# Second matrix of the three MLPs by block products of seven, first matrix's low parts by accumulating DMAs

## The chip, the cores and the metric

One core of one Trainium2 chip runs the kernel. The metric is the device time of one execution in microseconds; a kernel's time is the median of several runs. One execution was also recorded by the hardware profiler.

## What is computed

256 tokens of width 1024 pass through one block of a first kind and two of a second kind. Each block ends with an MLP of width 4096, and only these three MLPs change here:

```python
x = x + jnp.square(jax.nn.relu(h2 @ w_up[l])) @ w_down[l]              # first block
hid = jnp.square(jax.nn.relu(jnp.einsum('bsd,df->bsf', x, w_ff1)))     # each of the two others
ff = jnp.einsum('bsf,fd->bsd', hid, w_ff2)
return layernorm(DEEPNORM_ALPHA * x + ff, ln2_g, ln2_b)
```

All arrays are fp32. The first matrix is 1024x4096, the second 4096x1024.

## The kernel before

**Products in three parts.** Every fp32 operand is split into a high part, rounded to the engine's fp32r, and a low part, the rest. `mm3` (L319) then issues high x high, high x low and low x high: three matmuls (L320 to L322) for each block of 128 contracted rows.

**The weight stream.** All weights come from one packed array in the order of a plan (`build_plan`). A chunk is 128 x 2048 numbers and comes in two halves of 128x1024, 512 KB each. `Stream.load` has SP issue the loads into a ring of `RB` = 5 raw buffers. `Stream.piece` (L205) splits one half: ACT casts the raw half to the high part (`whi`, L213), then DVE subtracts it from the raw half to give the low part (`wlo`, L214). The split parts go to `NB` = 5 chunk buffers, and in an MLP `W.lend` adds a sixth. A chunk's buffer is free when PE has ended its last product with it (`W.free`).

**What sets the order.** The engines' queues are written in program order, with no scheduler. Between products the code calls `tick`, which advances the "sides" (generators with transposes and splits of other data) and pumps one or two pieces, if a buffer is free in program order. Each engine works its queue strictly in turn, so an instruction that waits holds all that stands behind it.

**An MLP.** Four chunks of the first matrix make hidden columns 0 to 1023 with the tokens on the partitions (these hidden columns are transposed by PE afterwards). The other twelve, here called up4 to up15, make 256 hidden columns each with the hidden columns on the partitions (`stream_a`): 48 matmuls of 128x256. ACT then applies relu and square (L800, L801), and the hidden block is split into high (ACT, L312) and low (DVE, L306). The second matrix is used in groups g of 512 hidden columns: `down(g, n, t, w)` multiplies the hidden block of token half t with the chunk of columns half n, 12 matmuls of 128x512. Each chunk serves both token halves, so 24 matmuls. The sums of all eight groups stay in four PSUM banks until the end, when `half` adds them to the residual in `xtok` and, in the second kind of block, makes the layer norm (`ln_half`, L912). Groups 0 to 5 run two groups behind up4 to up15, and groups 6 and 7 form a last round of four chunks, which are all held while each token half passes.

Of the kernel before, what the change touches and what calls it, by code (L numbers as in the profile page):

```python
# [9 lines left out]
F32 = mybir.dt.float32  # L10
# [6 lines left out]
D = 1024  # L17
S = 256
DFF = 4096
NB = 5  # L20
RB = 5
# [47 lines left out]

C2 = {}  # L70
# [7 lines left out]
def build_plan():  # L78

    plan = []  # L80
# [6 lines left out]

    def mlp(tag, wu, wd, l):
        for n in range(2):
            for j in range(2):  # L90
                wb((tag, "up", n, j), wu, l, 512 * n, 4 * j)
        for g in range(2, 8):
            for c in (2 * g, 2 * g + 1):
                wa((tag, "up", c), wu, l, 256 * c)
            for n in range(2):
                wb((tag, "dn", g - 2, n), wd, l, 512 * n, 4 * (g - 2))
        for n in range(2):
            for g in (6, 7):
                wb((tag, "dn", g, n), wd, l, 512 * n, 4 * g)
# [50 lines left out]

def pack_weights(inputs):

    plan = build_plan()
    flat = np.empty(sum(128 * k * n for _, _, _, _, k, _, n in plan), np.float32)
    o = 0
    for _, w, l, r0, k, c0, n in plan:
# [9 lines left out]
class Stream:  # L166
    def __init__(self, nc, raw_pool, w_pool, flat):
        self.nc, self.raw_pool, self.w_pool, self.flat = nc, raw_pool, w_pool, flat
        self.plan = [(p[0], p[4], p[6]) for p in build_plan()]
        self.dma_i = self.split_i = self.used = self.freed = self.off = 0  # L170
        self.raws, self.tiles = {}, {}
        self.main = []
        self.extra = None
        self.extra_used = -1

    def lend(self, pool, last):

# [1087 lines left out]
```

## Time and profile before

| | |
|---|---|
| Median of 3 runs | 1223.91 us (1223.78 to 1224.0) |
| The profiled execution's own time | 1223.95 us |
| Its span, first to last instruction | 1222.1 us |
| PE busy | 1208.5 us, 99% |
| DVE busy | 734.8 us, 60% |
| ACT busy | 631.6 us, 52% |
| DMA queue of SP (the weights) | 211.12 MB, 51.6% of 16 engines' span |
| Granted TensorE clock | 0.997 of 2.4 GHz |

A page of the profile gives the busy time of each engine and the chain of work that ended last, followed back from the last instruction. Groups of instructions have a line, an engine, an operation, output and input by name, their count, the busy sum, the mean of one, and the idle time before them with its releaser. The timeline has the start of each instruction or run of equal ones and how long it took. Matmuls overlap in the records, so their pace is read from start to start.

### The profile page before, as it was taken

Reading aid. Unit: us, or ns where it says so; the run is one execution under the profiler, and the core shown is the slowest. Engines: PE = TensorE matmul, PEld = TensorE weight load, DVE = VectorE, ACT = ScalarE, POOL = GpSimd, SP = SyncE. Lnnn points to the kernel's source line nnn. Section 1 sums busy time; section 2 is a strip of 40 time slices with the busy share of each in tenths; the row PEclk is TensorE's granted clock in tenths of the full one; section 3 lists DMA queues with packets and bytes.
Section 4 is the critical chain, followed back from the end, with each engine's and each line's share of the span. In section 5 each row is a group of like instructions: output and inputs, shape, how many; then the busy total and the mean of one; then the engine's idle time right before and its main releaser. Section 6 shows DMA issues by size and latency. Waiting matters only on the chain.

```text
span 1222.1 us, 18186 instructions
## 1 busy us (share of the span) xinstructions
PE 1208.5 (99%) x7365; PEld 1059.1 (87%) x7365; DVE 734.8 (60%) x941; ACT 631.6 (52%) x887; POOL 26.2 (2%) x45
## 2 busy tenths in 40 slices
PE   8999999999999999999999999999999999999997
PEld 5999987887888888998898889899889888989985
DVE  6488775656666655355476685535567668553452
ACT  6556555545454565455255556545535555653540
POOL 1000000000000000000000100000000010000000
PEclk9999999999999999999999999999999999999999
DMA  8644446665455565556444366555545436655530
GB/s 327 224 148 144 140 156 211 233 195 162 138 172 189 184 243 208 172 172 214 156 166 139 124 214 226 197 188 173 207 130 187 146 118 216 225 193 203 167 126 35
DMA packets 60468, 218.99 MB, mean 179 GB/s; under 512 B 6848, under 2 KB 6992, under 8 KB 60384
## 3 DMA queue, kind: packets, MB, share of 16 engines
q1 hardware_dynamic: 58320, 211.12, 51.6%
q0 software_dynamic: 1776, 6.38, 1.8%
q8 instruction: 58, 0.95, 0.3%
q10 hardware_dynamic: 288, 0.33, 0.1%
q14 instruction: 26, 0.21, 0.0%
HBM read 216.75 MB, written 1.05 MB: 178 GB/s over the span
## 4 chain that ended last, share of the span: by engine, by line
PE 95%; DVE 1%; ACT 1%; DMA 1%; issue 0%; DVEq 0%; POOLq 0%; SPq 0%; ACTq 0%
PE acc L320 17%; PE acc L322 17%; PE acc L321 17%; PE bank L320 13%; PE bank L322 13%; PE bank L321 13%; PE acc L402 2%; PE acc L333 2%; PE aux L329 1%; DMA raw<-in_wpack_dram 1%; PE aux L1082 0%; DMA gmix<-in_g_mix_dram 0%; DVE wlo L214 0%; PE aux L515 0%; PE aux L322 0%
## 5 line engine op out<-in xcount | busy, mean ns | idle before, releaser
L214 DVE TENSOR_TENSOR wlo<-raw,whi 128x1024 fp32r<-128x1024 f32 x392 | 465.0, 1221 | 116.6 <-ACT whi L213 114.5
L213 ACT CAST whi<-raw 128x1024 fp32r<-128x1024 f32 x392 | 394.6, 1048 | 108.7 <-PE bank L322 58.0
L320 PE MATMUL acc<-xTh,whi 128*128 128x256 f32 x1088 | 310.6, 285 | 0.0
L321 PE MATMUL acc<-xTl,whi 128*128 128x256 f32 x1088 | 307.7, 283 | 0.0
L322 PE MATMUL acc<-xTh,wlo 128*128 128x256 f32 x1088 | 307.5, 283 | 0.0
L320 PEld LDWEIGHTS acc<-xTh,whi 128*128 128x128 f32 x1088 | 207.9, 191 | 2.7 <-issue 1.0
L321 PEld LDWEIGHTS acc<-xTl,whi 128*128 128x128 f32 x1088 | 207.9, 191 | 1.0
L322 PEld LDWEIGHTS acc<-xTh,wlo 128*128 128x128 f32 x1088 | 208.0, 191 | 0.0
L320 PE MATMUL bank<-whi,hid 128*128 128x512 f32 x384 | 151.4, 394 | 0.0
L322 PE MATMUL bank<-whi,hid 128*128 128x512 f32 x384 | 151.3, 394 | 0.0
L321 PE MATMUL bank<-wlo,hid 128*128 128x512 f32 x384 | 151.2, 394 | 0.0
L306 DVE TENSOR_TENSOR hid<-r,hid 128x512 fp32r<-128x512 f32 x36 | 24.9, 692 | 166.2 <-ACT hid L312 166.2
L800 ACT ACTIVATE r<-acc 128x512 f32<-128x512 f32 x36 | 21.5, 598 | 147.1 <-PE acc L322 147.1
L320 PE MATMUL acc<-whi,xTh 128*128 128x512 f32 x224 | 90.6, 404 | 0.7 <-ACT xTh L312 0.7
L321 PE MATMUL acc<-wlo,xTh 128*128 128x512 f32 x224 | 88.2, 394 | 1.1 <-DVE wlo L214 1.1
L322 PE MATMUL acc<-whi,xTl 128*128 128x512 f32 x224 | 88.3, 394 | 0.0
L322 PEld LDWEIGHTS bank<-whi,hid 128*128 128x128 f32 x384 | 72.2, 188 | 16.9
L320 PEld LDWEIGHTS bank<-whi,hid 128*128 128x128 f32 x384 | 72.3, 188 | 15.9
L321 PEld LDWEIGHTS bank<-wlo,hid 128*128 128x128 f32 x384 | 72.2, 188 | 16.0
L320 PE MATMUL bank<-whi,xTh 128*128 128x512 f32 (+2 forms) x192 | 68.7, 358 | 0.0
L321 PE MATMUL bank<-wlo,xTh 128*128 128x512 f32 (+2 forms) x192 | 68.1, 354 | 0.0
L322 PE MATMUL bank<-whi,xTl 128*128 128x512 f32 (+2 forms) x192 | 68.0, 354 | 0.0
(263 smaller groups left out, 1457.6 us busy)
## 6 DMA issues: line engine op xcount, KB each, us to landing
raw<-in_wpack_dram SPq DMA_DIRECT2D x388, 512.0 KB, 4.4
raw<-in_wpack_dram SPq DMA_DIRECT2D x4, 528.0 KB, 4.3
gb<-in_ln_g_dram POOLq DMA_DIRECT2D x4, 512.0 KB, 3.9
bb<-in_ln_b_dram POOLq DMA_DIRECT2D x4, 512.0 KB, 6.1
x<-in_x_dram SPq DMA_DIRECT2D x3, 512.0 KB, 7.0
mem<-in_mem_dram SPq DMA_DIRECT2D x2, 512.0 KB, 6.5
out_dram<-x SPq DMA_DIRECT2D x4, 256.0 KB, 2.2
cst<-in_c_dram POOLq DMA_DIRECT2D x1, 898.0 KB, 7.0
```

Of the source, the lines that this page charges most:

```text
L213: nc.scalar.copy(hi, raw)
L214: nc.vector.tensor_tensor(lo, raw, hi.bitcast(F32), op=ALU.subtract)
L306: nc.vector.tensor_tensor(o, x, y, op=op)
L320: nc.tensor.matmul(o, lhsT=lh, rhs=rh, start=first, stop=False, skip_group_check=True)
L321: nc.tensor.matmul(o, lhsT=lh, rhs=rl, start=False, stop=False, skip_group_check=True)
L322: nc.tensor.matmul(o, lhsT=ll, rhs=rh, start=False, stop=last, skip_group_check=True)
L329: nc.tensor.matmul(o[:, h, :], lhsT=q[a][hs[h]], rhs=k[b][hs[h]], start=i == 0, stop=i == 2, skip_group_check=True)
L333: nc.tensor.matmul(o, lhsT=l, rhs=r, start=first, stop=last, skip_group_check=True)
L402: nc.tensor.transpose(o[:, k * 128:(k + 1) * 128], src[:, k * 128:(k + 1) * 128], ident)
L800: nc.scalar.activation(dst, src, AF.Relu)
```

## The change

The second matrix is cut, for each pair of groups (1024 hidden columns, "pair" 0 to 3), into four quarters of 512x512: q0 and q1 of the first group (columns half 0, half 1), q3 and q2 of the second. In pairs 0 and 2 the four outputs (two token halves by two column halves) are made of seven block products instead of eight. `PRODUCTS` lists them in their order: 1, 5, 6, 3, 7, 2, 4, here P1, P5, P6, P3, P7, P2, P4. Each has a chunk of its own, made of the raw quarters: P1 is q0, P5 is q0 = q0 + q1, P6 is q0 = q0 + q2, P3 is q2, P7 is q1 = q1 + q2, P2 is q3, P4 is q3 = q3 + q0. The sums are made in place in the raw buffers by DVE (`Stream.add`, L234). Each product also has an operand of its own, made from the hidden quarters (`seven_side`: four differences on DVE, seven splits on ACT and DVE). A product is 12 matmuls of 128x512. P1, P6, P7 and P4 accumulate on one PSUM bank ("A"), P5 and P3 on a second ("C"), P2 has a third ("B"). After each product `gather` adds or subtracts the bank as it then stands to a block of `xtok` (a DVE instruction with `xtok` and the bank as inputs, L353), so the next product on that bank comes after the gather. Pairs 1 and 3 keep the eight products; pair 1 is gathered into `xtok` too, pair 3 ends in `half`.

The order of an MLP is now: four first chunks; up4 to up7; seven products of pair 0; up8 to up11; the four chunks of pair 1; up12 to up15; seven products of pair 2; the four chunks of pair 3.

For the halves of up4 to up15, DVE makes no low part any more. ACT writes the negated high part into `wlo` (L251), and GpSimd issues a DMA (L252) that reads the weights again from the packed array and adds them onto `wlo`. The raw half is then free after ACT's cast.

`NB` is 4 in place of 5, with no lent buffer, and `RB` is 8 in place of 5. The four quarters of a pair are eight raw halves and stay in the ring until their last use.

```diff
-NB = 5
-RB = 5
+NB = 4
+RB = 8
...
+PRODUCTS = ((1, 0, None), (5, 0, 1), (6, 0, 2), (3, 2, None), (7, 1, 2), (2, 3, None), (4, 3, 0))
...
+    def w7(key, w, l, k0, c0, c1):
+        quarters = [(w, l, 128 * (k0 + 4 * i), 4, (c0, c1)[j], 512) for i, j in ((0, 0), (0, 1), (1, 1), (1, 0))]
+        for name, q, s in PRODUCTS:
+            plan.append(((*key, name), quarters if q == 0 and s is None else None, q, s))
...
-        for g in range(2, 8):
-            for c in (2 * g, 2 * g + 1):
+        for pair in range(1, 4):
+            for c in range(4 * pair, 4 * pair + 4):
                 wa((tag, "up", c), wu, l, 256 * c)
+            if pair % 2:
+                w7((tag, "dn", pair - 1), wd, l, 8 * (pair - 1), 0, 512)
             for n in range(2):
-                wb((tag, "dn", g - 2, n), wd, l, 512 * n, 4 * (g - 2))
-        for n in range(2):
-            for g in (6, 7):
-                wb((tag, "dn", g, n), wd, l, 512 * n, 4 * g)
+                for g in (2, 3) if pair == 2 else (6, 7) if pair == 3 else ():
+                    wb((tag, "dn", g, n), wd, l, 512 * n, 4 * g)
...
-    def lend(self, pool, last):
-
-        self.extra = (pool, [p[0] for p in self.plan].index(last))
-        self.extra_used = -1
-
-    def slot(self, c):
-        if self.extra is not None and c <= self.extra[1] and self.extra_used < self.freed:
-            return 2
-        return 1 if len(self.main) < NB or self.main[-NB] < self.freed else 0
...
-        return c < len(self.plan) and (h == 1 or self.slot(c) > 0)
+        return c < len(self.plan) and (h == 1 or c < NB + self.freed)
...
+        while self.dma_i < 2 * len(self.loads):
+            i, h = divmod(self.dma_i, 2)
+            j, g = divmod(self.dma_i - upto, 2)
+            if j >= 0 and 2 * self.last[j] + g >= self.split_i:
+                return
...
+    def add(self):
+        if self.added == self.split_i and self.added < 2 * len(self.plan):
+            c, h = divmod(self.added, 2)
+            _, _, _, q, s = self.plan[c]
+            if s is not None:
+                a, b = self.raws[2 * q + h], self.raws[2 * s + h]
+                self.nc.vector.tensor_tensor(a, a, b, op=ALU.add)
+            self.added += 1
     def piece(self):
         nc = self.nc
         c, h = divmod(self.split_i, 2)
-        m = self.plan[c][1] * self.plan[c][2] // 2
+        _, k, n, q, _ = self.plan[c]
+        m = k * n // 2
         if h == 0:
-            p = self.w_pool
-            if self.slot(c) == 2:
-                p, self.extra_used = self.extra[0], c
-            else:
-                self.main.append(c)
-            self.tiles[c] = tuple(p.tile([128, WMAX], F32R, tag=t, name=t) for t in ("whi", "wlo"))
+            self.tiles[c] = tuple(self.w_pool.tile([128, WMAX], F32R, tag=t, name=t) for t in ("whi", "wlo"))
         hi, lo = (t[:, h * m:(h + 1) * m] for t in self.tiles[c])
-        raw = self.raws.pop(self.split_i)
+        self.add()
+        raw = self.raws[2 * q + h]
         nc.scalar.copy(hi, raw)
-        nc.vector.tensor_tensor(lo, raw, hi.bitcast(F32), op=ALU.subtract)
         self.split_i += 1
+        self.add()
+        if self.by_dma(self.plan[c][0]):
+            nc.scalar.mul(lo, hi.bitcast(F32), -1.0)
+            nc.gpsimd.dma_start(lo, self.srcs[2 * q + h], accum_op=ALU.add)
+        else:
+            nc.vector.tensor_tensor(lo, raw, hi.bitcast(F32), op=ALU.subtract)
         self.load()
+    @staticmethod
+    def by_dma(key):
+        return len(key) == 3 and key[1] == "up"
...
+        def seven_side(pair):
+            x = hf[pair]
+            q = {(i, j): x[:, 4 * j:4 * j + 4, 128 * i:128 * i + 128] for i in range(2) for j in range(2)}
+            r = hp.tile([128, D], F32, tag="r", name="r", bufs=2)
+            d, e = (r[:, 512 * i:512 * i + 512].rearrange("p (k t) -> p k t", k=4) for i in range(2))
+            def put(name, src):
+                o = new_op(7)
+                split(o[0], o[1], src)
+                ops[pair, name] = o
+            put(1, q[0, 0])
+            tt(d, q[1, 1], q[1, 0], ALU.subtract)
+            yield
+            put(5, d)
+            stt(e, d, -1.0, q[0, 0], ALU.mult, ALU.subtract)
+            yield
+            put(6, e)
+            stt(d, e, -1.0, q[0, 1], ALU.mult, ALU.subtract)
+            yield
+            put(3, d)
+            tt(e, q[0, 0], q[1, 0], ALU.subtract)
+            yield
+            put(7, e)
+            yield
+            put(2, q[0, 1])
+            yield
+            put(4, q[1, 1])
...
+        def gather(i, j, bank, op):
+            x = xtok[:, i, 512 * j:512 * j + 512]
+            stt(x, x, alpha if (i, j) not in first else 1.0, bank, ALU.mult, op)
+            first.add((i, j))
+        def seven(pair):
+            bk = {}
+            for name, _, _ in PRODUCTS:
+                while (pair, name) not in ops:
+                    tick(0)
+                x = ops[pair, name]
+                c = "A" if name in (1, 6, 7, 4) else "B" if name == 2 else "C"
+                fresh = c not in bk
+                if fresh:
+                    bk[c] = bank()
+                w = W.get((tag, "dn", pair, name))
+                for k in range(4):
+                    mm3(bk[c], x[0][:, k, :], x[1][:, k, :], w[0][:, k, :], w[1][:, k, :], fresh and k == 0, k == 3)
+                    if k == 1:
+                        tick()
+                W.free()
+                for i, j, op in {1: ((0, 0, ALU.add),), 5: ((1, 1, ALU.subtract),), 6: ((0, 1, ALU.subtract),),
+                                 3: ((0, 1, ALU.subtract),), 7: ((1, 1, ALU.subtract),), 2: ((0, 0, ALU.add),),
+                                 4: ((1, 0, ALU.add),)}[name]:
+                    gather(i, j, bk[c], op)
+                tick()
...
+        for pair in range(1, 4):
+            for c in range(4 * pair, 4 * pair + 4):
+                p = stream_a((tag, "up", c), xT)
...
+            if pair % 2:
+                seven(pair - 1)
+            if pair == 2:
+                for n in range(2):
+                    p = [bank(), bank()]
+                    for g in (2, 3):
+                        w = W.get((tag, "dn", g, n))
+                        for t in range(2):
+                            down(p[t], n, g, t, w)
+                            if t:
+                                W.free()
+                            if g == 3:
+                                gather(t, n, p[t], ALU.add)
+                            tick()
```

In the counts of the two programs, matmuls of 128x512 on `bank` go from 1920 to 1848. On DVE, low parts of weights (128x1024) go from 388 to 352, 48 sums of raw halves (128x1024) are new, instructions on `xtok` with a bank (128x512) go from 24 to 78, and in place of 48 low parts of hidden blocks (128x512) stand 42 of 128x512 and 48 of 128x256 with 24 differences (128x512). On ACT, casts of weights go from 388 to 424, and 72 negated copies (128x1024) are new. On GpSimd 72 DMAs are new. SP's loads stay 392.

DVE around the first products of the second matrix in the first MLP. Before, from the split of up5's hidden block to that of up6's:

```order
L306 TENSOR_TENSOR hid_4083<-r,hid_4082 128x512 [waits Activation_49]
L214 TENSOR_TENSOR wlo<-raw,whi 128x1024 [waits DMAHW7_49,Activation_49]
L214 TENSOR_TENSOR wlo<-raw,whi 128x1024 [waits DMAHW0_49,Activation_49]
L214 TENSOR_TENSOR wlo<-raw,whi 128x1024 [waits DVE_49,DMAHW1_49,PE_49,Activation_49]
L214 TENSOR_TENSOR wlo<-raw,whi 128x1024 [waits DMAHW2_49,Activation_49]
L214 TENSOR_TENSOR wlo<-raw,whi 128x1024 [waits DMAHW3_49,DVE_49,Activation_49]
L214 TENSOR_TENSOR wlo<-raw,whi 128x1024 [waits DMAHW4_49,Activation_49]
L306 TENSOR_TENSOR hid_4301<-r,hid_4300 128x512 [waits PE_49,Activation_49]
```

Now, from the sum of P7's first half to the third gather (`x_3502<-x_3502,bank` rows are gathers, `raw<-raw` rows are sums of raw halves, `op` rows are splits of operands):

```order
L234 TENSOR_TENSOR raw<-raw 128x1024
L254 TENSOR_TENSOR wlo<-raw,whi 128x1024 [waits Activation_49]
L353 SCALAR_TENSOR_TENSOR x_3502<-x_3502,bank 128x512 [waits PE_49]
L350 TENSOR_TENSOR op_4390<-hf,op_4390 128x512 [waits Activation_49]
L234 TENSOR_TENSOR raw<-raw 128x1024
L254 TENSOR_TENSOR wlo<-raw,whi 128x1024 [waits Activation_49] x2
L353 SCALAR_TENSOR_TENSOR x_3502<-x_3502,bank 128x512 [waits PE_49]
L254 TENSOR_TENSOR wlo<-raw,whi 128x1024 [waits DMAHW1_49,Activation_49]
L234 TENSOR_TENSOR raw<-raw 128x1024 [waits DVE_49]
L254 TENSOR_TENSOR wlo<-raw,whi 128x1024 [waits DMAHW2_49,Activation_49]
L353 SCALAR_TENSOR_TENSOR x_3502<-x_3502,bank 128x512 [waits PE_49]
```

Before, nothing on DVE read a PSUM bank among these products; now a gather that waits for PE stands between the splits and sums, behind those that the code pumped earlier.

DVE at the end of the first MLP's second set of seven. Before, from the split of up15's hidden block into the last round:

```order
L306 TENSOR_TENSOR hid_5093<-r,hid_5092 128x512 [waits Activation_49]
L214 TENSOR_TENSOR wlo<-raw,whi 128x1024 [waits DMAHW7_49,Activation_49]
L214 TENSOR_TENSOR wlo<-raw,whi 128x1024 [waits DMAHW0_49,Activation_49]
L214 TENSOR_TENSOR wlo<-raw,whi 128x1024 [waits DVE_49,DMAHW1_49,PE_49,Activation_49]
L214 TENSOR_TENSOR wlo<-raw,whi 128x1024 [waits DMAHW2_49,Activation_49]
```

Now, from the sum for P4's second half to the gather of P2 (the gathers here are those of P3, P7 and P2):

```order
L234 TENSOR_TENSOR raw<-raw 128x1024 [waits DVE_49]
L254 TENSOR_TENSOR wlo<-raw,whi 128x1024 [waits Activation_49] x2
L353 SCALAR_TENSOR_TENSOR x_3502<-x_3502,bank 128x512 [waits PE_49]
L254 TENSOR_TENSOR wlo<-raw,whi 128x1024 [waits DMAHW3_49,Activation_49]
L254 TENSOR_TENSOR wlo<-raw,whi 128x1024 [waits DMAHW4_49,Activation_49]
L353 SCALAR_TENSOR_TENSOR x_3502<-x_3502,bank 128x512 [waits PE_49]
L254 TENSOR_TENSOR wlo<-raw,whi 128x1024 [waits DMAHW5_49,Activation_49]
L254 TENSOR_TENSOR wlo<-raw,whi 128x1024 [waits DMAHW6_49,Activation_49]
L353 SCALAR_TENSOR_TENSOR x_3502<-x_3502,bank 128x512 [waits PE_49]
```

Two low parts for the first chunk of pair 3, with loads of their own to wait for, now stand between the gather of P3 and that of P7.

ACT at the splits of the chunks up8 and up9 in the first MLP. Before:

```order
L312 CAST hid_4498<-r 128x512 [waits Activation_49]
L213 CAST whi<-raw 128x1024 [waits DMAHW5_49]
L213 CAST whi<-raw 128x1024 [waits DMAHW6_49]
L800 ACTIVATE r<-acc 128x512 [waits DVE_49,PE_49]
L801 ACTIVATE r<-r 128x512 [waits Activation_49]
L312 CAST hid_4498<-r 128x512 [waits Activation_49]
```

Now, behind the casts of P4's halves:

```order
L247 CAST whi<-raw 128x1024 [waits DVE_49]
L247 CAST whi<-raw 128x1024 [waits DMAHW3_49,PE_49,Activation_49]
L251 ACTIVATE wlo<-whi 128x1024 [waits DMASW7_49,DMASW6_49,Activation_49]
L247 CAST whi<-raw 128x1024 [waits DMAHW4_49]
L251 ACTIVATE wlo<-whi 128x1024 [waits Activation_49]
L247 CAST whi<-raw 128x1024 [waits DMAHW5_49,PE_49]
L251 ACTIVATE wlo<-whi 128x1024 [waits DMASW1_49,DMASW0_49,Activation_49]
```

Each half of these chunks has a second ACT instruction, and GpSimd's queue has one DMA for each; here from up8's first half to up10's first half:

```order
L252 DMA wlo<-in_wpack_dram 128x1024 [waits DMASW0_49,DMASW6_49,DVE_49,DMASW7_49,PE_49,Activation_49]
L252 DMA wlo<-in_wpack_dram 128x1024 [waits DMASW1_49,Activation_49]
L252 DMA wlo<-in_wpack_dram 128x1024 [waits DVE_49,DMASW2_49,PE_49,Activation_49]
L252 DMA wlo<-in_wpack_dram 128x1024 [waits DMASW3_49,Activation_49]
L252 DMA wlo<-in_wpack_dram 128x1024 [waits DVE_49,DMASW4_49,PE_49,Activation_49]
```

A half of up8 is whole when this DMA has landed, where before it was whole after DVE's subtraction.

## Rows read from the trace of the kernel before

**Rows 1.** The page: busy us, share and instructions of each engine; PE clock by slice.

```profile
PE 1208.5 (99%) x7365; PEld 1059.1 (87%) x7365; DVE 734.8 (60%) x941; ACT 631.6 (52%) x887; POOL 26.2 (2%) x45
...
PEclk9999999999999999999999999999999999999999
```

**Rows 2.** The page: the chain that ended last, shares of the span by engine.

```profile
PE 95%; DVE 1%; ACT 1%; DMA 1%; issue 0%; DVEq 0%; POOLq 0%; SPq 0%; ACTq 0%
```

**Rows 3.** Waits of PE, longest in total first: us in total, times, longest us.

```profile
PE acc L402 <- DVE ht L309: 1.3, 1, 1.3
PE acc L321 <- DVE wlo L214: 1.1, 1, 1.1
```

**Rows 4.** Stretches in the first two MLPs: length, busy us (instructions) by engine, clock, DMA share, GB/s.

```profile
440.00:620.00 180.00, 180.00 (x1116) 161.68 (x1115) 92.18 (x99) 86.70 (x108) 0.54 (x1) 1.00 0.52 176
700.00:890.00 190.00, 190.00 (x1127) 168.19 (x1126) 106.72 (x115) 103.04 (x130) 2.19 (x4) 1.00 0.60 204
```

**Rows 5.** Timeline of PE in the first MLP: start us, us, what, count.

```profile
442.08 0.29 PE L320 MATMUL acc<-xTh,whi 128*128 128x256 f32 x1
...
447.85 0.28 PE L320 MATMUL acc<-xTh,whi 128*128 128x256 f32 x1
...
450.72 1.03 PE L402 MATMUL acc<-ident,r 128*128 128x128 f32 x8
451.51 0.36 PE L320 MATMUL acc<-xTh,whi 128*128 128x256 f32 x1
...
454.46 0.39 PE L320 MATMUL bank<-whi,hid 128*128 128x512 f32 x1
...
460.96 0.39 PE L321 MATMUL bank<-wlo,hid 128*128 128x512 f32 x1
```

**Rows 6.** Groups by line and shape: count, busy us, mean ns of one, idle before.

```profile
L214 DVE TENSOR_TENSOR wlo<-raw,whi 128x1024 fp32r<-128x1024 f32 x388 | 460.1, 1220 | 116.0 <-ACT whi L213 113.8
L213 ACT CAST whi<-raw 128x1024 fp32r<-128x1024 f32 x388 | 390.4, 1048 | 106.2 <-PE bank L322 58.0 <-issue 15.9 <-PE acc L322 15.9
L306 DVE TENSOR_TENSOR hid<-r,hid 128x512 fp32r<-128x512 f32 x36 | 24.9, 692 | 166.2 <-ACT hid L312 166.2
L916 DVE SCALAR_TENSOR_TENSOR x<-x,bank 128x512 f32<-128x512 f32 x16 | 11.0, 684 | 30.2 <-PE bank L322 30.2
L306 DVE TENSOR_TENSOR mixl<-acc,mixh 128x256 fp32r<-128x256 f32 x8 | 3.4, 422 | 5.0 <-ACT mixh L312 4.7
L801 ACT ACTIVATE r<-r 128x512 f32<-128x512 f32 x48 | 30.4, 633 | 1.5
L800 ACT ACTIVATE r<-acc 128x512 f32<-128x512 f32 x36 | 21.5, 598 | 147.1 <-PE acc L322 147.1
L312 ACT CAST mixh<-acc 128x256 fp32r<-128x256 f32 x8 | 3.0, 373 | 14.7 <-PE acc L333 14.7
```

**Rows 7.** Timeline of DVE in the first MLP.

```profile
452.38 1.29 DVE L306 TENSOR_TENSOR hid<-acc,hid 128x512 fp32r<-128x512 f32 x2 [0.20 <-ACT hid L312]
...
457.56 5.76 DVE L214 TENSOR_TENSOR wlo<-raw,whi 128x1024 fp32r<-128x1024 f32 x5 [0.26 <-ACT whi L213]
```

**Rows 8.** DMA issues: out<-in queue op xcount, KB each, median us to landing.

```profile
raw<-in_wpack_dram SPq DMA_DIRECT2D x388, 512.0 KB, 4.4
gb<-in_ln_g_dram POOLq DMA_DIRECT2D x4, 512.0 KB, 3.9
bb<-in_ln_b_dram POOLq DMA_DIRECT2D x4, 512.0 KB, 6.1
```

**Rows 9.** Stretches at the kernel's start: as rows 4.

```profile
6.00:10.00 4.00, 2.19 (x12) 0.95 (x10) 2.32 (x5) 1.84 (x5) 0.55 (x1) 0.99 1.02 408
10.00:20.00 10.00, 8.71 (x32) 6.12 (x32) 8.85 (x10) 6.97 (x10) 2.30 (x4) 0.83 1.00 386
```

**Rows 10.** Timeline of PE at the kernel's start.

```profile
12.30 0.63 PE L321 MATMUL acc<-wlo,xTh 128*128 128x512 f32 x1
12.73 0.63 PE L322 MATMUL acc<-whi,xTl 128*128 128x512 f32 x1
```

More of the change, by code (lines that the diff above doesn't have):

```diff
@@ L148, in build_plan, with build_loads @@
     return plan
+def build_loads():
+    loads, chunks = [], []
+    for p in build_plan():
+        if len(p) == 7:
+            chunks.append((p[0], p[4], p[6], len(loads), None))
+            loads.append(p[1:])
+            continue
+        key, quarters, q, s = p
+        if quarters is not None:
+            base = len(loads)
+            loads.extend(quarters)
+        chunks.append((key, 4, 512, base + q, None if s is None else base + s))
+    return loads, chunks
 def pack_weights(inputs):
-    plan = build_plan()
-    flat = np.empty(sum(128 * k * n for _, _, _, _, k, _, n in plan), np.float32)
+    loads = build_loads()[0]
+    flat = np.empty(sum(128 * k * n for _, _, _, k, _, n in loads), np.float32)
     o = 0
-    for _, w, l, r0, k, c0, n in plan:
+    for w, l, r0, k, c0, n in loads:
         for h in range(2):
@@ L186, in room @@
+        self.last = [0] * len(self.loads)
+        for c, (_, _, _, q, s) in enumerate(self.plan):
+            self.last[q] = c
+            if s is not None:
+                self.last[s] = c
+        self.dma_i = self.split_i = self.added = self.used = self.freed = self.off = 0
+        self.raws, self.srcs, self.tiles = {}, {}, {}
     def room(self):
         c, h = divmod(self.split_i, 2)
-        return c < len(self.plan) and (h == 1 or self.slot(c) > 0)
+        return c < len(self.plan) and (h == 1 or c < NB + self.freed)
@@ L786, in block_kernel, with mlp @@
     yst.close()
-    def mlp(tag, xT, half, on_start):
+    def mlp(tag, xT, half, on_start, xtok, alpha):
         st = ExitStack()
@@ new lines, in mlp @@
+        first = set()
+        def gather(i, j, bank, op):
[23 more added lines that the diff above has]
+                tick()
@@ L910, in cc_, with ln_half @@
         return c2s["cst"][:, C2[n][0]:C2[n][1]]
-    def ln_half(t, n, bank, xtok, gb, bb, xT, cell, tmp, fin=None):
+    def ln_half(t, n, bank, xtok, gb, bb, xT, cell, tmp, fin=None, alpha=ALPHA):
         ns = slice(512 * n, 512 * n + 512)
@@ L915, in ln_half @@
             cell[t] = sm.tile([128, 2], F32, tag="lsum", name="lsum")
-        nc.vector.scalar_tensor_tensor(out=xtok[:, t, ns], in0=xtok[:, t, ns], scalar=ALPHA, in1=bank, op0=ALU.mult,
+        nc.vector.scalar_tensor_tensor(out=xtok[:, t, ns], in0=xtok[:, t, ns], scalar=alpha, in1=bank, op0=ALU.mult,
                                        op1=ALU.add, accum_out=cell[t][:, n:n + 1])
@@ L1221, in mlp_half @@
                 ln_half(t, n, bank, xtok, gb2[0], gb2[1], None, cellf, tmp,
[L1222 removed]
+                        lambda t, hs: nc.sync.dma_start(out[0, t * 128:(t + 1) * 128, hs], xtok[:, t, hs]), 1.0)
                 return
```

88 lines of the change are left out of this document (44 added, 44 removed).

## The prediction, made before the changed kernel was run

> **What bounds the kernel now.** I read the page's busy shares first: PE works 1208.5 us of 1222.1, at the full clock in every slice [rows 1]. The chain that ended last is PE for 95% [rows 2], and PE's waits for other engines are single ones of 1.3 us and less [rows 3]. Then the stretches inside the MLPs: PE is busy 180.00 us of 180, while DVE has 92.18 and ACT 86.70 [rows 4]. So in an MLP the time is the number of matmuls times their pace. DVE and ACT have room on average; whether they have it at each place is another question, and the change puts their work in bursts.
>
> The pace comes from starts [rows 5]: 48 matmuls of 128x256 take 447.85 - 442.08 = 5.77 us, one chunk of up4 to up15. Of 128x512, 28 take 460.96 - 454.46 = 6.50 us, 0.232 each, so a product of 12 takes 2.79. Eight transposes take 0.79.
>
> **What is removed.** 1920 - 1848 = 72 matmuls of 128x512, all on the path: 72 x 0.232 = 16.7 us.
>
> **DVE's prices.** Alone: 1.220 us for a low part (128x1024), 0.692 for 128x512, 0.684 for the form of a gather, 0.422 for 128x256 [rows 6]. In a row they are closer: five low parts in 5.76 us are (5.76 - 1.22)/4 = 1.14 apart, two of 128x512 in 1.29 are 0.60 apart [rows 7]. I take 1.14, 0.60 (gathers too) and 0.34 for 128x256, less by the same 0.08. The sum of two raw halves is not in the trace; L214 has its shape and two fp32 inputs, so 1.14 to 1.22, and 1.14 is taken. Over the kernel DVE gets 36 x 1.22 fewer, 48 x 1.22 + 54 x 0.684 + 42 x 0.692 + 24 x 0.692 + 48 x 0.422 more, less 48 x 0.692: about 85 us more, 820 in all. That would still hide on average. It doesn't hide around the sevens.
>
> **The first seven (pair 0).** P1 takes the buffer of up4, four chunks earlier, so its split can't begin before PE has ended up4; call that time 0. PE then has up5 to up7 and eight transposes, 3 x 5.77 + 0.79 = 18.1, and without a wait P7, the fifth product, would start at 18.1 + 4 x 2.79 = 29.3. P7 adds onto bank A and so waits for P6's gather. By DVE's order there stand, from 0 to the end of P1's gather, 8 low parts and 5 sums (13 x 1.14 = 14.8), 10 operand instructions of 128x512 (6.0), 8 splits of 128x256 (2.7) and the gather (0.6): 24.1. DVE also stands still in it. The splits of up4's and up5's hidden blocks come in program order and need ACT's 0.60 + 0.63 + 2 x 0.37 = 2.0 us [rows 6] after PE has ended those chunks. The first costs 2.0; the second is reached at about 7.2 and ready at 8.2; short waits for casts bring it to 4.4 in all. So P1's gather ends at 28.5. PE has ended P5 at 23.7 and stands **4.8** before P6 (bank A). Then DVE has an operand split, a sum, two low parts and P5's gather (0.60 + 3 x 1.14 + 0.60 = 4.6): 33.1, while P6 ends at 31.3, so P3 (bank C) waits **1.8**. A low part, a sum, a low part and P6's gather (4.0) end at 37.1, P3 at 35.9: P7 waits **1.2**. P2 and P4 find all ready. Together 7.8 us.
>
> ACT has 22.8 us of work in those 28.5 (4 x 1.23 for relu and square, 8 x 0.37, 9 of 128x512 at 0.60, 9 casts of 1.05), so it runs just ahead of DVE and I charge it nothing. If DVE were faster, ACT would be next.
>
> **The second seven (pair 2).** Time 0 is the end of up12. The operands are made by then. Up to P6's gather DVE has 12 low parts and 7 sums (21.7), 8 splits (2.7) and three gathers (1.8): 26.2. It stands longer, as each pair of small splits waits for the relu of the chunk that PE has just ended: 2.0, 1.0, 0.6, 1.7 and two short ones, 6.2 in all. That is 32.4, against 3 x 5.77 + 4 x 2.79 = 28.5 for PE: 3.9 late. Then P4 (bank A) needs P7's gather, and ahead of it on DVE stand the two low parts of pair 3's first chunk. Its raw halves go into q0's buffers, whose last use is the sum for P4. The second of these sums ends at 32.4 + 1.1 = 33.5; a load takes 4.4 us [rows 8], the cast 1.05, the low part 1.22, the gather 0.68: 40.9. P4 could have started at 32.4 + 2 x 2.79 = 38.0: 2.9 late. Together 6.8 us.
>
> **up8 after the first seven.** Its raw halves wait for the same buffers. The second is free after the second sum for P4, at 37.1 + 1.1 = 38.2, lands at 42.6, and has its cast and its negated copy (taken as a cast, 1.05) at 44.7. Then comes the accumulating DMA, D. PE reaches up8 at 37.1 + 3 x 2.79 = 45.5 and that half's low part 14 matmuls later, at 47.2. So PE waits D - 2.5, or nothing. No transfer of the trace accumulates. The nearest rows are plain ones of the same size on GpSimd's queue: 3.9 and 6.1 us, the second issued right behind another [rows 8]. Here they are issued in pairs beside a burst of eight loads, and they read their destination too, so I take 6.1: **3.6 us**. The low end is 1.4; the high end, twice 6.1, is 9.7. At that end up4 is late as well: its buffer comes free 3 x 2.79 + 0.79 = 9.2 before PE needs it, two casts and two copies take 4.2, so D over 6.7 shows, 5.5 us at 12.2.
>
> The Trainium skill (DMA: Bandwidth & Descriptors, Anatomy of one DMA) gives a DMA from GpSimd about 2.0 us plus its bytes at 436 GB/s, an estimate of 3.2 us for 512 KB. By that the wait would be 0.7 and the sum 8.7 us lower; rows 8 show more even for a plain one.
>
> **At nothing.** With `NB` 4 three chunks still lie ahead, 17 us in streams of 128x256 against some 4 for a split; with four held, the next has 8 us. SP's loads are the same number. If that cover is thin in the attention stages, it costs a few us. It can't gain.
>
> **The sum.** The profiled execution's own time, 1223.95, is the median 1223.91 but for 0.04. 1223.95 - 16.7 + 3 x (7.8 + 6.8 + 3.6) = 1223.95 - 16.7 + 54.6 = **1261.9**.
>
> **Rivals.**
> - *DVE keeps up (faster).* Then gathers wait for PE and not PE for gathers, and what stays is the 16.7, less at most 3 x 3.6 for up8: 1207 to 1218. It decides at 29.3 us of DVE time to P6's gather in pair 0. I count 32.7 without any standing; five low parts would have to be 0.96 apart instead of 1.14 [rows 7]. For it speaks only that DVE's mean share is low.
> - *DVE late, but standing less.* Without the standing, pair 0 costs 32.7 - 29.3 = 3.4, pair 2 only P4's 2.9: with 1.4 to 3.6 for up8, 1230 to 1237. Half way is 1250.
> - *The accumulating DMAs are the bound.* With D = 12.2, 3 x (6.1 + 5.5) = 35 more: 1297. The 4 MB that the ring could not load during a seven come in one burst with 4 MB of accumulations; the start of the kernel moved 408 and 386 GB/s at a full DMA share [rows 9], so 8 MB take over 20 us there, close to PE's 23 for four chunks. A higher price of an accumulated byte makes it the bound.
> - *The clock falls.* At the start PE was busy 2.19 us of 4, and in the next stretch the granted clock was 0.83 [rows 9], with matmuls 0.43 apart: the level of 1.2 GHz [rows 10]. After the 4.8 us before P6 the same may come. P6 at 12 x 0.43 = 5.2 would end at 33.7 against P5's gather at 33.1, so 0.6 shows; on P2 and P4, where nothing hides it, 2.4 each. 1264 to 1277. The Trainium skill (TensorE: Matmul & The Clock Gate, Part 1) says that the throttled level is the default and activity releases it; rows 9 and 10 agree. By that rule the fall before P6 is likely, and its time is this rival's.
>
> That the products are not saved is ruled out by the count of matmuls.
>
> **How the numbers follow.** The forecast, 1250 to 1264, has 0.43; the clock 0.15; slow accumulations 0.20, of which 0.07 lie over 1300; less standing 0.13; faster 0.07; a balance at no change 0.02. The likeliest time is 1262. From 1238 to 1300 leaves out the 0.07 and 0.02, some 0.04 of the less standing and 0.07 above: 0.20. A measurement can tell 0.2% from no change: slower 0.91, same 0.02, faster 0.07.
>
> **What would show it.** Right: PE's waits for DVE's instructions on `xtok` (L353) come to 12 to 15 us in each MLP, the longest near 5 us and before P6; between the gathers DVE has no idle; PE waits a few us for the DMAs onto `wlo` at up8. The time from issue to landing of L252 gives D. Wrong: gathers that stand idle for PE; PE waits in up5 to up7 or in the attention stages; a clock under 0.99 in the MLPs.

## The result and the profile after

The changed kernel takes 1315.93 us (median; 1315.17 to 1316.62) against 1223.85 in the same runs: 1.075 times as long [1.073, 1.077]. Slower, as forecast, but 54 us above the forecast of 1262 and outside its range, which ended at 1300.

The page of the changed kernel answers to [rows 1] and [rows 2]: busy us, share and instructions of PE; its clock by slice; the DMA queues (packets, MB, share of 16 engines); the chain that ended last.

```profile
PE 1224.1 (93%) x7293; PEld 1062.9 (81%) x7293; DVE 806.4 (61%) x1073; ACT 760.7 (58%) x1049; POOL 87.7 (7%) x117
...
PEclk9999999999999998999999999899999999989999
...
q1 hardware_dynamic: 58320, 211.12, 47.4%
q0 software_dynamic: 12144, 44.14, 16.1%
...
PE 65%; DMA 16%; DVE 7%; issue 6%; ACT 4%; POOL 1%; POOLq 0%; DVEq 0%; SPq 0%; ACTq 0%
```

72 matmuls are gone (7365 to 7293), yet PE is busy 15.6 us longer, 32 more than the count of its matmuls gives. Some 17 of these are matmuls at the lower clock (below); what the rest is, is not shown. DMA, 1% of the chain before, is 16% of it.

PE's waits in the changed kernel, longest in total first (us, times, longest us), where [rows 3] had single ones of 1.3 and less; then the DMAs of L252, issue to landing:

```profile
PE acc L366 <- DMA wlo<-in_wpack_dram: 46.1, 28, 5.8
PE bank L364 <- DVE x L353: 20.7, 12, 3.3
PE bank L364 <- ACT whi L247: 8.2, 7, 1.6
```

```profile
DMA to landing us min/median/max: 6.0/13.1/23.1
```

In the sevens the view puts some of PE's waits down to ACT's cast. Every one of these waits, whatever its name, ends 0.15 us after a gather has ended, so all of them are waits for gathers: 20.7 + 8.2 = 28.9 us.

Three stretches of the first MLP, as in [rows 4]: up4 to up7, the first seven, up8 to up11 (length, busy us and instructions of PE, PEld, DVE, ACT, POOL, then clock, DMA share, GB/s):

```profile
442.00:474.00 32.00, 27.19 (x204) 26.10 (x203) 16.53 (x22) 26.86 (x38) 4.27 (x6) 0.95 0.86 220
476.00:498.00 22.00, 16.37 (x69) 12.46 (x68) 20.30 (x24) 14.26 (x17) 1.09 (x2) 1.00 0.57 184
499.00:531.00 32.00, 23.64 (x154) 22.36 (x153) 5.41 (x5) 17.02 (x20) 5.11 (x6) 0.84 1.05 277
```

The two DMA queues in the last stretch (packets, MB, share of 16 engines), q0 being GpSimd's and q1 SP's:

```profile
q0 software_dynamic: 1144, 4.19, 65.8%
q1 hardware_dynamic: 1269, 4.62, 38.7%
```

In the middle stretch DVE is the engine that works (20.3 of 22). In the last one none is full but the DMA engines, with a share of 1.05, and DVE has 5.4 of 32: the place where the change freed DVE is a place where DVE had nothing to do. The 4.19 MB of q0 are eight accumulations, the 4.62 MB of q1 some nine loads. In the first stretch the DMA share is 1.05 as well until 466 us, and 0.29 behind that.

The timeline of PE shows where it stands in these stretches (start us, us, what, idle before):

```profile
443.52 0.39 PE L366 MATMUL acc<-xTh,wlo 128*128 128x256 f32 x1 [0.69 <-DMA wlo<-in_wpack_dram]
...
447.22 0.53 PE L366 MATMUL acc<-xTh,wlo 128*128 128x256 f32 x1 [2.01 <-DMA wlo<-in_wpack_dram]
...
482.52 0.48 PE L364 MATMUL bank<-whi,op 128*128 128x512 f32 x1 [2.88 <-DVE x L353]
...
487.20 0.47 PE L364 MATMUL bank<-whi,op 128*128 128x512 f32 x1 [1.64 <-ACT whi L247]
...
504.81 0.39 PE L366 MATMUL acc<-xTh,wlo 128*128 128x256 f32 x1 [4.63 <-DMA wlo<-in_wpack_dram]
...
508.81 0.58 PE L366 MATMUL acc<-xTh,wlo 128*128 128x256 f32 x1 [1.48 <-DMA wlo<-in_wpack_dram]
```

The first two are up4's halves, then P6 and P3, then up8's halves. Each chunk and product is measured from its first matmul to the first one of the next. Less the pace of [rows 5] (for up5, 6.62 with its transposes), that gives what each stage is late, in us:

| Stage | forecast per MLP | MLP 1 | MLP 2 | MLP 3 |
|---|---|---|---|---|
| up4 | 0 | 4.7 | 5.1 | 5.2 |
| up5 to up7 | 0 | 2.9 | 2.6 | 2.2 |
| first seven | 7.8 | 6.4 | 6.4 | 6.7 |
| up8 | 3.6 | 8.9 | 10.2 | 9.4 |
| up9 to up11 | 0 | 4.9 | 4.2 | 4.4 |
| up12 to up15 | 0 | 1.2 | 2.7 | 1.2 |
| second seven | 6.8 | 5.8 | 5.8 | 5.8 |

The sevens come to 37 us, the chunks that wait for accumulations to 70; 1222.1 - 16.7 + 107 = 1312, of a span of 1314.8.

### The profile page after: what moved, and what is told of

The parts are those of the page before. It is cut to its first block, busy times and chain, and to the rows that moved or that the text cites. A ratio compares the mean times of both kernels' runs of the same rounds, so it can differ in the third digit from the quotient of the medians.

```text
span 1314.8 us, 18509 instructions
## 1 busy us (share of the span) xinstructions
PE 1224.1 (93%) x7293; PEld 1062.9 (81%) x7293; DVE 806.4 (61%) x1073; ACT 760.7 (58%) x1049; POOL 87.7 (7%) x117
## 3 DMA queue, kind: packets, MB, share of 16 engines
q1 hardware_dynamic: 58320, 211.12, 47.4%
q0 software_dynamic: 12144, 44.14, 16.1%
HBM read 254.50 MB, written 1.05 MB: 194 GB/s over the span
## 4 chain that ended last, share of the span: by engine, by line
PE 65%; DMA 16%; DVE 7%; issue 6%; ACT 4%; POOL 1%; POOLq 0%; DVEq 0%; SPq 0%; ACTq 0%
DMA wlo<-in_wpack_dram 14%; PE acc L366 11%; PE acc L364 11%; PE acc L365 11%; PE bank L364 8%; PE bank L365 8%; PE bank L366 8%; DVE wlo L254 3%; PE acc L377 2%; ACT whi L247 2%; DVE raw L234 1%; PE acc L446 1%; POOL wlo L252 1%; PE aux L373 1%; DMA raw<-in_wpack_dram 1%
## 5 line engine op out<-in xcount | busy, mean ns | idle before, releaser
L254 DVE TENSOR_TENSOR wlo<-raw,whi 128x1024 fp32r<-128x1024 f32 (+1 forms) x356 | 426.8, 1221 | 148.5 <-ACT whi L247 147.3
L247 ACT CAST whi<-raw 128x1024 fp32r<-128x1024 f32 x428 | 436.1, 1047 | 141.4 <-DVE raw L234 53.1
L366 PE MATMUL acc<-xTh,wlo 128*128 128x256 f32 x1088 | 318.4, 293 | 46.6 <-DMA wlo<-in_wpack_dram 46.1
L364 PE MATMUL bank<-whi,op 128*128 128x512 f32 x360 | 145.2, 403 | 29.1 <-DVE x L353 20.7
L366 PE MATMUL bank<-whi,op 128*128 128x512 f32 x360 | 143.2, 398 | 0.0
L365 PE MATMUL bank<-wlo,op 128*128 128x512 f32 x360 | 143.1, 397 | 0.0
L364 PEld LDWEIGHTS bank<-whi,op 128*128 128x128 f32 x360 | 68.6, 191 | 52.3 <-ACT whi L247 33.1
L350 DVE TENSOR_TENSOR op<-r,op 128x256 fp32r<-128x256 f32 (+1 forms) x72 | 34.2, 509 | 115.3 <-ACT op L356 115.3
L252 POOL DMA_DIRECT2D wlo<-in_wpack_dram x72 | 61.3, 852 | 351.0 <-ACT wlo L251 233.3
L366 PEld LDWEIGHTS bank<-whi,op 128*128 128x128 f32 x360 | 68.5, 190 | 16.1
L365 PEld LDWEIGHTS bank<-wlo,op 128*128 128x128 f32 x360 | 68.7, 191 | 14.8
L251 ACT ACTIVATE wlo<-whi 128x1024 fp32r<-128x1024 f32 x72 | 76.3, 1059 | 2.3
## 6 DMA issues: line engine op xcount, KB each, us to landing
wlo<-in_wpack_dram POOLq DMA_DIRECT2D x72, 512.0 KB, 13.1
```

The source lines that it names most:

```text
L247: nc.scalar.copy(hi, raw)
L251: nc.scalar.mul(lo, hi.bitcast(F32), -1.0)
L252: nc.gpsimd.dma_start(lo, self.srcs[2 * q + h], accum_op=ALU.add)
L254: nc.vector.tensor_tensor(lo, raw, hi.bitcast(F32), op=ALU.subtract)
L350: nc.vector.tensor_tensor(o, x, y, op=op)
L364: nc.tensor.matmul(o, lhsT=lh, rhs=rh, start=first, stop=False, skip_group_check=True)
```

## Experiments

Theory: the kernel is 92 us longer; the sevens are late by some 40 us, through DVE, and the rest of the lateness is the accumulating DMAs, which cost more than I took. Rival: the clock. Nine times PE runs at the lower of its two levels (1.2 in place of 2.4 GHz) behind such a wait. Its matmuls of 128x256 are then 0.22 us apart in place of 0.12, as here behind up4's wait, and over all nine this adds up to some 17 us.

```profile
448.83 0.41 PE L364 MATMUL acc<-xTh,whi 128*128 128x256 f32 x1
449.05 0.41 PE L365 MATMUL acc<-xTl,whi 128*128 128x256 f32 x1
```

**No accumulating DMAs, all low parts on DVE.**

```diff
     def by_dma(key):
-        return len(key) == 3 and key[1] == "up"
+        return False
```

> The changed kernel, but DVE makes the low parts of up4 to up15 again; the products of seven, the sums, the gathers, NB 4 and RB 8 stay. Theory (two costs: accumulating DMAs that fill the DMA engines, and DVE late at the sevens): the waits for wlo DMAs and the half-clock stretches go; DVE also has up8's low parts ahead of P7's gather in the first seven; 1255 to 1265 us, PE's waits at the sevens 45 to 55 us in all. Rival A (the products of seven cost what is lost): 1290 or more. Rival B (the ring of raw buffers, held by the quarters, makes up8 late whoever makes its low part): up8 still waits over 4 us, 1270 to 1285.

1255.53 us, 1.026 [1.025, 1.028]. PE's waits in it:

```profile
PE bank L364 <- DVE x L353: 25.2, 12, 5.1
PE bank L364 <- ACT whi L247: 10.2, 10, 1.1
```

The time is as expected: without the DMAs and their negated copies 60 us of the 92 are gone, and what is left is +32. PE's waits in the sevens are 35 us (25.2 + 10.2, all for gathers), under the 45 to 55 expected. By stage, with slow matmuls counted, the first seven is 9.8 us late in each MLP (P6 5.2), the second 5.9, up4 to up15 not at all; 3 x 15.7 - 16.7 = 30. So the ring of raw buffers does not make up8 late. The DMAs give back 60 us where the table has 70, since PE now comes to the sevens on time and stands there 10 us longer.

**Accumulating DMAs alone, in the kernel before.**

```diff
-        nc.vector.tensor_tensor(lo, raw, hi.bitcast(F32), op=ALU.subtract)
+        key = self.plan[c][0]
+        if len(key) == 3 and key[1] == "up":
+            nc.scalar.mul(lo, hi.bitcast(F32), -1.0)
+            nc.gpsimd.dma_start(lo, self.srcs[self.split_i], accum_op=ALU.add)
+        else:
+            nc.vector.tensor_tensor(lo, raw, hi.bitcast(F32), op=ALU.subtract)
```

> The kernel before, with its eight products, buffers and ring, and the low parts of up4 to up15 made by accumulating DMAs. Theory: an accumulating half needs some 2.6 us of all 16 DMA engines where a load needs 1.3, so a round of two up chunks and four others fills 21 of 22.7 us; the look-ahead hides most of it: 1225 to 1245 us, DMA busy share in the MLPs over 0.85. Rival A (the DMAs cost nothing by themselves, only with the sevens' bursts): 1222 to 1226. Rival C (an accumulation has a long latency that no look-ahead here hides): over 1270.

1230.93 us, 1.006 [1.004, 1.008]. Its largest wait of PE, and its DMAs:

```profile
PE bank L327 <- ACT xTh L319: 4.1, 3, 1.6
```

```profile
wlo<-in_wpack_dram POOLq DMA_DIRECT2D x72, 512.0 KB, 9.3
```

The time lies in the theory's range, at its low end. No wait for these DMAs, though the median one takes 9.3 us. From 440 to 620 us PE is busy 180.00 of 180, at a DMA share of 0.84. There the chunks up4 to up15 come two at a time between chunks of the second matrix, with five or six buffers. What shows is 7 us, in part ACT, which the negated copies keep from the MLP's first operands. So the DMAs cost 60 us beside the sevens and 7 without. The full engines of the stretches above point to the bursts; the changed kernel also has fewer buffers, and no run tells what five or six would have saved there.

**Plain copies in place of accumulations.**

```diff
-            nc.gpsimd.dma_start(lo, self.srcs[2 * q + h], accum_op=ALU.add)
+            nc.gpsimd.dma_start(lo, self.srcs[2 * q + h])
```

> The changed kernel with the 72 DMAs copying the weights over wlo instead of adding them, so the low parts of up4 to up15 are not low parts; bytes from HBM and order are the same. Theory (the accumulated byte is dear): issue to landing falls from 13.1 to 6 to 9 us, PE's waits for wlo at up4 to up15 fall by more than half, 1265 to 1290 us. Rival C (the second read of the weights and GpSimd's queue are what is slow): landing 11 us or more, 1305 to 1316.

1280.46 us, 1.046. Queue, DMAs and waits:

```profile
q0 software_dynamic: 12144, 44.14, 10.2%
...
wlo<-in_wpack_dram POOLq DMA_DIRECT2D x72, 512.0 KB, 7.6
```

```profile
PE bank L364 <- DVE x L353: 32.2, 12, 7.9
PE acc L366 <- DMA wlo<-in_wpack_dram: 13.0, 8, 3.6
```

As expected. The queue also gives the price, as engine time. The q0 queue without these DMAs takes 1.6% of 1259.4 = 20 us of all 16 engines (the row of q0 of the copy-only kernel below). With copies it takes 10.2% of 1279.2 = 130, so a copy is 110 / 72 = **1.53** us of all engines. With accumulations it takes 16.1% of 1314.8 = 212, so an accumulation is 192 / 72 = **2.7**. A load of SP's is 47.4% of 1314.8 us over 211.12 MB, 1.55 for 512 KB.

**Accumulations of half the size.**

```diff
-            nc.gpsimd.dma_start(lo, self.srcs[2 * q + h], accum_op=ALU.add)
+            nc.gpsimd.dma_start(lo[:, :m // 2], self.srcs[2 * q + h][:, :m // 2], accum_op=ALU.add)
```

> The changed kernel with each accumulating DMA on half of its columns (256 KB instead of 512); the other half of these low parts is left out and stays the negated high part. If the time of these DMAs is their bytes on shared engines, the time from issue to landing falls from 13.1 to 5 to 8 us, PE's 46 us of waits for them go to 0 to 15 and the time is 1262 to 1285, near the 1280.5 of plain copies of full size. If it is a fixed cost of an accumulating DMA, it stays at 10 us or more and the time is 1295 or more.

1278.35 us in one run. Waits and DMAs:

```profile
PE acc L366 <- DMA wlo<-in_wpack_dram: 11.3, 4, 3.8
```

```profile
wlo<-in_wpack_dram POOLq DMA_DIRECT2D x72, 256.0 KB, 6.9
...
q0 software_dynamic: 12144, 25.26, 9.9%
```

As expected: half the bytes, half the time to landing (6.9 for 13.1), and 38 us given back, about as many as by plain copies (35). By the same working an accumulation of half the size takes 1.5 us of all engines. So what these DMAs cost goes with their bytes and is no fixed cost of each, and it shows where the engines are full.

**PE kept busy before up4 and up8.**

```diff
         p = acc()
+        for i in range({4: 32, 8: 64}.get(key[2], 0) if len(key) == 3 and key[1] == "up" else 0):
+            mm(pv[:, 0, :], x[0][:, 0, 0:128], x[0][:, i % 8, :])
```

> The changed kernel with matmuls of no use put into the accumulator that is about to be started: 32 of 128x256 (3.8 us) ahead of up4 and 64 (7.7 us) ahead of up8, where PE stands 4.7 to 5.2 and 8.9 to 10.2 us longer than its pace. If the clock that falls after these waits is a cost of its own, the stretches at half clock behind up4 and up8 vanish and with them what they cost, 1.4 and 2.2 to 3.0 us in each MLP, some 12 in all: 1301 to 1308. If the accumulating DMAs set the pace there, a faster PE only waits longer in up5 to up7 and up9 to up11: 1312 to 1318.

1318.97 us, 1.078 [1.076, 1.080]. The stretches of up4 to up7 and up8 to up11, columns as above, and the longest wait:

```profile
442.00:474.00 32.00, 29.33 (x237) 28.58 (x236) 16.16 (x21) 26.70 (x38) 4.24 (x6) 1.00 0.87 221
499.00:531.00 32.00, 28.03 (x226) 27.25 (x225) 5.41 (x5) 18.01 (x22) 5.12 (x6) 1.00 1.05 276
```

```profile
PE acc L366 <- DMA wlo<-in_wpack_dram: 27.2, 26, 1.9
```

The clock is 1.00 in both stretches (0.95 and 0.84 without these matmuls), half-clock matmuls cost 6 us in place of 17, and the time is not shorter by any of it; it is 1 us over the second range expected. DMA share and GB/s are the same within 1 in the last digit, and PE, which is now faster, stands longer behind up8 for the next low parts (up9 to up11 are 5.3 to 5.8 us late for 4.2 to 4.9). At the chunks that wait for DMAs the clock rival falls: PE slowed down where it had time to. Behind P6's wait the clock still fell; this run does not test that place.

**The DMA left out, the negated copy kept.**

```diff
             nc.scalar.mul(lo, hi.bitcast(F32), -1.0)
-            nc.gpsimd.dma_start(lo, self.srcs[2 * q + h], accum_op=ALU.add)
```

> The changed kernel with the negated copies on ScalarE but without the DMAs behind them: the low parts of up4 to up15 stay the negated high parts. DVE has 72 low parts fewer than in the kernel with no DMAs (1255.5), and nothing waits for a transfer. If these low parts are not among those that make DVE late in the sevens (there stand the low parts of P1 to P4), nothing is gained, and the copies keep ScalarE from the operands: P6 late by 7 to 8 us as with plain copies, 1255 to 1268. If the relief of DVE counts, its waits at the sevens fall well below 25 us and the time is 1225 to 1248.

1261.15 us, 1.030 [1.028, 1.032]. Waits (the lines stand one lower) and the queue q0:

```profile
PE bank L363 <- DVE x L352: 35.7, 12, 8.8
PE bank L363 <- ACT whi L247: 6.8, 7, 1.1
```

```profile
q0 software_dynamic: 1776, 6.38, 1.6%
```

DVE makes 72 low parts fewer than in the first experiment, nothing waits for a transfer, and the kernel is 5.6 us slower. The timelines say why. First the kernel without DMAs: ACT's split of up4's hidden block and DVE's; then the same two here.

```profile
449.52 0.71 ACT L356 CAST op<-r 128x256 fp32r<-128x256 f32 x2
```

```profile
449.96 0.76 DVE L350 TENSOR_TENSOR op<-r,op 128x256 fp32r<-128x256 f32 x2 [2.89 <-ACT op L356]
...
476.13 0.67 DVE L353 SCALAR_TENSOR_TENSOR x<-x,bank 128x512 f32<-128x512 f32 x1
```

```profile
454.45 0.71 ACT L355 CAST op<-r 128x256 fp32r<-128x256 f32 x2
```

```profile
454.88 0.76 DVE L349 TENSOR_TENSOR op<-r,op 128x256 fp32r<-128x256 f32 x2 [24.95 <-ACT op L355]
...
480.16 0.68 DVE L352 SCALAR_TENSOR_TENSOR x<-x,bank 128x512 f32<-128x512 f32 x1
```

ACT still has casts and negated copies of up6 and up7 ahead of that split, so everything on DVE up to P1's gather comes 4 to 5 us later, after DVE has stood 25 us for ACT. P6 is late by 9.0, 8.1 and 8.1 us, against 5.2. The low parts that went were not in DVE's late stretch ahead of P6; there stand those of the seven products' chunks, which are still its own. In one place they did count: in the kernel without DMAs, up8's first two stand ahead of P7's gather, and P4 is 1.3 us late for it in each MLP; here it is on time. P6's 9.4 us more in all, less these 3.9, are the 5.6 us.

**Half of the DMAs, on chunks that lie further ahead.**

```diff
-        return len(key) == 3 and key[1] == "up"
+        return len(key) == 3 and key[1] == "up" and key[2] % 4 > 1
```

> The changed kernel with accumulating DMAs for up6, up7, up10, up11, up14 and up15 alone, 36 of the 72; the other low parts on DVE. If the accumulations hurt by their bulk beside the bursts of loads (13.1 us from issue to landing with 72), half of them come to 6 to 9 us and nearly vanish from PE's waits, since these chunks lie two buffers ahead: 1235 to 1252, between none (1255.5) and less, since DVE loses 36 low parts. If each accumulation is slow whatever the company, PE still waits for them, 12 us or more in all, and the time is 1255 to 1290.

1260.40 us, 1.030 [1.028, 1.031].

```profile
PE bank L364 <- DVE x L353: 25.0, 12, 5.1
PE bank L364 <- ACT whi L247: 10.2, 10, 1.1
PE acc L366 <- DMA wlo<-in_wpack_dram: 3.0, 4, 1.6
```

```profile
DMA to landing us min/median/max: 7.7/11.0/16.1
```

Between the two answers: the time is the second's, the waits for DMAs (3.0 us) are the first's. The time from issue to landing falls only from 13.1 to 11.0, which I put down to the four in a row that still meet the loads; that is not shown. The total is no better than without DMAs, and PE waits for gathers as long as there (25.0 and 25.2): a second sign that the low parts of up6 and up7 did not stand in the sevens' way.

**Sums of the raw quarters on 64 of 1024 columns**, first in the changed kernel, then also without DMAs.

```diff
-                self.nc.vector.tensor_tensor(a, a, b, op=ALU.add)
+                self.nc.vector.tensor_tensor(a[:, :64], a[:, :64], b[:, :64], op=ALU.add)
```

> The changed kernel with the sums of raw halves made on 64 of 1024 columns, so the weights of P5, P6, P7 and P4 are wrong elsewhere; all waits and buffers stay. Theory (DVE's work ahead of the gathers makes PE wait): each sum falls from 1.14 to some 0.15 us, PE's waits at P6, P3 and P7 fall from 36 us in all to under 8, part of it comes back as longer waits at up8: 1280 to 1298 us. Rival D (the round trip from PE to a gather and back makes the wait): the waits stay over 25 us, 1305 to 1316.

1291.22 us, 1.055, as expected: PE's waits named by gathers fall from 20.7 to 5.7 us, those for DMAs stay (46.0).

> The changed kernel without accumulating DMAs, and with the sums of raw halves made on 64 of 1024 columns, so that the weights of four of the seven products are left out in part: the sums then cost DVE nearly nothing. If the sums are what makes DVE late, PE's waits for gathers fall from 25 us to 0 to 10 and the time is 1207 to 1225. If the low parts and operand work alone make DVE late, 1225 to 1245.

1225.53 us in one run, at the edge between the two answers; the waits are the first's.

```profile
PE bank L364 <- DVE x L353: 5.6, 3, 1.9
PE bank L364 <- DVE raw L234: 2.1, 3, 0.7
PE bank L364 <- ACT whi L247: 1.9, 3, 0.6
```

The sums are 30 of the 47 us that the sevens are late without DMAs. The other 17 remain (3.7 in each first seven, 1.9 in each second), and 72 matmuls save as much: with sums for nearly nothing the kernel comes within 2 us of the kernel before.

**Sums on GpSimd, no DMAs.**

```diff
-                self.nc.vector.tensor_tensor(a, a, b, op=ALU.add)
+                self.nc.gpsimd.tensor_tensor(a, a, b, op=ALU.add)
```

> The changed kernel without accumulating DMAs (all low parts on DVE), and with the sums of raw halves on GpSimd instead of DVE. The theory that DVE's work in the sevens is what is left without the DMAs (1255.5, 25 us of PE's waits for gathers) says that 48 x 1.14 us less on DVE shortens these waits: with narrow sums they went from about 6.3 to 3.7 us per first seven and from 5.8 to 2.5 per second, so 1225 to 1240. The rival, that GpSimd's sum is so slow that the cast behind it comes late, says PE's waits name whi or the sums' line and the time is 1245 to 1300.

1289.56 us, 1.053 [1.052, 1.055]. The time is the rival's, the mechanism neither's: PE waits for DVE more than in any other version, and the 13.7 us put down to ACT's cast also end 0.15 us after a gather.

```profile
PE bank L364 <- DVE x L353: 50.2, 6, 11.4
```

GpSimd's and DVE's timelines:

```profile
466.24 7.81 POOL L234 TENSOR_TENSOR raw<-raw 128x1024 f32<-128x1024 f32 x3 [1.76 <-DVE wlo L254]
```

```profile
466.08 5.77 DVE L350 TENSOR_TENSOR op<-r,op 128x256 fp32r<-128x256 f32 x3
471.77 2.83 DVE L353 SCALAR_TENSOR_TENSOR r<-r,hf 128x512 f32<-128x512 f32 x1
```

A sum is 2.6 us on GpSimd, and while three of them run (466.24 to 474.05), DVE's three splits take 5.77 us in place of 1.35 and the next instruction 2.83 in place of 0.68. The Trainium skill (SBUF — State Buffer, SBUF: two separate sides) calls the port pair that the two share an exclusive lock: against a GpSimd instruction that reads SBUF, a DVE instruction with two inputs there blocks until the other has ended. The rows agree.

**Four weight tiles, eight raw halves, nothing lent, in the kernel before.**

```diff
-NB = 5
-RB = 5
+NB = 4
+RB = 8
```

> The kernel before with four weight tiles and eight raw halves, and without the two lent tiles in the MLPs; nothing else of the change. My prediction charged this part at nothing. If that holds, 1222 to 1228. If the thinner cover shows (casts or loads that come late in the attention stages or at the MLP starts), 1228 to 1245, with PE's waits for whi, wlo or raw naming the place.

1224.75 us, 1.0007 [0.9998, 1.0016]: nothing, as charged, with eight products and no DMAs.

## Why the prediction was wrong

**The step that failed is the term D of up8**, in its size and in its place. I took 6.1 us from issue to landing, from a plain DMA behind another one [rows 8], with 12.2 as the high end. It measured 13.1 (6.0 to 23.1). The first fault is the price: an accumulation keeps the 16 engines 2.7 us where a load of the same size keeps them 1.55. The second is the shape of the term: I charged one latency at one place, up8, where the burst is a matter of throughput. Around up8 to up11 stand eight accumulations and some eight loads: 8 x 2.7 + 8 x 1.55 = 34 us of full engines, against 23 of PE's work. That is 11 late, and up8 to up11 measured 13.8, 14.4 and 13.8. So the lateness did not stop at up8, and up4 to up7 got a smaller one of the same kind (7.4 to 7.7). With up12 to up15 these are 70 us where 11 were forecast: all of the miss, and a little more. The forecast had named PE's waits in up5 to up7, and a clock under 0.99, as signs that it was wrong; both came.

**The rival that came true** is that the accumulating DMAs are the bound (given 0.20). Its mechanism was right, to the burst of loads and accumulations beside each other, and so were its two terms: with D = 12.2 it had up8 and up4 late by 3 x (9.7 + 5.5) = 46 us, and they measured 43.5. Its time, 1297, was too short above all because the other chunks, up5 to up7 and up9 to up15, stood at nothing there too; they are the other 26 us. Its working on the burst used the GB/s of plain loads [rows 9] and left a higher price of an accumulated byte as a condition, which held: the stretch moved 277 GB/s at a full DMA share, where [rows 9] had 386.

**DVE's terms were right in size, less so in place.** In the kernel without DMAs PE comes to the sevens on time, as the forecast supposed. P1's gather ended at 476.80 there, 28.8 us after up4's end at 448.0; worked out were 28.5. P6 was 5.2 late (4.8), P3 2.5 (1.8), P7 0.8 (1.2). P4's 1.3 there belongs to up8's low parts, which DVE makes in that kernel and not in the changed one. P3 in fact waited for no gather in the first two MLPs. In the first, the starts of P6 and P3, and P5's gather, are

```profile
476.95 0.76 PE L364 MATMUL bank<-whi,op 128*128 128x512 f32 x1 [5.05 <-DVE x L353]
...
482.21 0.63 PE L364 MATMUL bank<-whi,op 128*128 128x512 f32 x1
```

```profile
480.80 0.68 DVE L353 SCALAR_TENSOR_TENSOR x<-x,bank 128x512 f32<-128x512 f32 x1
```

P6 ran at the lower clock and took 5.26 us, and P5's gather was over at 481.48: 0.7 us of P3's lateness is the clock, as that rival had it (0.6). The second seven was 5.9 late (6.8), but not where I had put it: P6 1.9, P3 1.3, P7 1.3 and P4 1.3, for P7 3.9 and P4 2.9. Together, without P4's 1.3 in the first sevens, 43 us for 44. That the two sums agree so well is in part luck.

**ACT was charged at nothing, and that was wrong**, though it did not show in the sum: with the copies alone P6 is 8 to 9 us late. My 22.8 us of ACT's work behind the end of up4 had no negated copy in them; up7's two came there. In the changed kernel PE itself is 7 to 8 us late by then, which is why its first seven, at 6.4 to 6.7, looks better than forecast. ACT's copies and PE's own lateness, both left out there, work against each other.

**The clock** fell behind the waits of up4 and of chunks from up8 to up11, and in the second and third MLP behind P6's, the one place that the rival had named for it; the rows of the first MLP say 0.95 and 0.84. Behind up4 and up8 its price was not to be added: on a stretch that the DMAs pace, a full clock returned nothing. The 16.7 us of removed matmuls and the zero for the buffers hold; so does the sign.

None of these versions beats the kernel before. What stays open is a kernel with the sums done at no cost to DVE and the remaining 17 us of lateness removed as well; its gain could be 16.7 us at most.

## What to carry to other kernels

Before work is moved off an engine, look whether that work stands in the stretch where the engine is late: most of the 72 low parts left DVE where it had time, and ACT and the DMA engines took the load where they had none. Price a burst of transfers as a sum of engine time over the stretch against the consumer's work in it, not as one latency at the first consumer. And a block product saved is worth only its matmuls (2.8 us here), so the additions that it needs must fit under them.

## What was not expected of the hardware

- An accumulating DMA from DRAM onto SBUF costs the DMA engines 2.7 us for 512 KB, 1.7 times a plain copy from the same queue (1.53).
- A full clock on TensorE can be worth nothing: 0.84 and 1.00 over the same 32 us gave the same progress, at a DMA share of 1.05 in both.
- GpSimd's sum of two fp32 tiles takes 2.6 us for 128x1024, against 1.22 on DVE, and while three of them ran, three two-input instructions on DVE took 5.77 us in place of 1.35.
